# Input projection of a hybrid RWKV-7 / short-convolution block: other columns for the split weights, other pieces, and two pieces in turns

## The chip, the cores and the metric

The kernel runs on one core of one Trainium2 chip. The metric is the time of one execution on the device, in microseconds (us). Before the change the median of three runs is 1019.06 us (1018.99 to 1020.0). Times inside a run come from the hardware profiler's record of one execution.

## The reference

The layer prepends 16 learned tokens to 512 real ones (528 positions, model width 2048), normalises, and multiplies by one input matrix with 8320 columns. Group A (r, k, v, a gate g and two low-rank columns, here "lora") goes through a token shift and a delta-rule recurrence over 16 heads; group B (B, C, h and a gate gc) through a width-3 causal convolution. Both go through one output projection, a residual and a last norm.

```python
hn = _rmsnorm(h_res, norm_in_g[l])
P = hn @ w_in[l]                                   # (528, 2048) @ (2048, 8320)
...
y_a = (yn + bonus.reshape(bsz, L, D_RWKV)) * jax.nn.silu(g_r)
...
y_b = Bg * _causal_depthwise_conv(Cg * hc, conv_w[l]) * jax.nn.silu(g_c)
mix = jnp.concatenate([y_a, y_b], axis=-1)
h_res = h_res + mix @ w_out[l]
out = _rmsnorm(h_res, norm_f_g)
```

Everything is float32.

## The kernel before

**Precision.** A float32 product is made of three matmuls on a reduced format (fp32r): both operands are split into a high part and a low remainder, and high x high, high x low and low x high are added up in PSUM. `xh` and `xl` are the parts of the normalised input, kept in SBUF for the whole projection; they are laid out as [128, 16, 576], one row of 576 columns for each of the 16 blocks of 128 input features, of which columns 0 to 527 hold the positions (0 to 15 the learned tokens).

**Tiles of the projection.** The 8320 output columns make 65 tiles of 128: eight each of r, k, v, g, B, C, h, gc, and one lora. A tile is the product of its 2048 x 128 weights with the input: 16 blocks of features x 3 products. The weights are the stationary operand, the input is the moving one. The positions that a kind needs are cut into pieces, each with its own PSUM bank: `FULL` (k, v, lora) is 0 to 256 and 256 to 528, `TAIL` (r, g, C, h; these start two positions ahead of the first real one) is 14 to 270 and 270 to 528, `REAL` (B, gc) is one piece of 512 from 16 on. So a tile has 96 matmuls, or 48 for B and gc.

**Weights.** `prefetch` (lines 142 to 150 of the kernel) loads half a tile's weights by DMA and has them split in quarters of four feature blocks: ScalarE writes the high part (line 138), VectorE or GpSimd the low one (line 139). `parts_of` puts both into one SBUF tile of 1088 columns, six of which rotate: the high part takes 512 columns from a starting column `SHIFT[kind]` on, the low part the 512 after it. `SHIFT` is thus the place of the weights in their tile, in columns of 4 bytes; it changes nothing in what is computed. For the output projection the same tiles hold the moving operand, at `SHIFT["out"]`.

**Order.** The order on TensorE is written out by hand. `mains` is a generator over the tiles in the order of `plan`; its first stretch runs lora 0, k 0, r 0 and B 0 block by block together, and from the fifth tile on each tile goes through `main`. `main` runs over the four quarters; in each, `steps` runs the first piece over four blocks and three products (12 matmuls, line 326), then the second piece under the same weights again. Every matmul that is yielded adds an estimate of 0.43 ns a column to a clock; small work of the recurrence is put in between by `fill(ns)`, which draws tiles from `mains` until the estimate is used up, and deferred DMAs are issued by the same clock. The first block of lora (line 484) is the one place where the two pieces follow each other under the same weights. After a tile its PSUM banks are read by VectorE (`scaled`, line 345). `pm` rotates four banks for the tiles.

**After the projection** the output product runs over units of 24 matmuls of 512 columns (line 1231), with its own weights prefetched, added and split on the way; the last gc tile's result is needed for it.

Of the kernel before, what the change touches and what calls it, by code (L numbers as in the profile page):

```python
# [18 lines left out]
P = 128  # L19
DM = 2048  # L20
KT = DM // P
SEQ = 512
META = 16
L = SEQ + META
# [50 lines left out]


LX = 576
SHIFT = {"lora": 16, "k": 16, "v": 32, "r": 30, "C": 30, "h": 62, "B": 16, "g": 30, "gc": 0, "out": 40}


@with_exitstack
def hymba_kernel(ctx: ExitStack, tc: tile.TileContext, xt, xtok, front, w_in, w_out, pv, lup, cst, msk, gf, out):
    nc = tc.nc
# [39 lines left out]
    quarters, chain, low = {}, {}, {}  # L123
# [4 lines left out]
    def parts_of(kind, name):  # L128
        t = wp.tile([P, 2 * 512 + 64], F32R, tag="hl", name=name, bufs=6)
        o = SHIFT[kind]  # L130
        return t[:, o : o + 512], t[:, o + 512 : o + 1024]

    def kind_of(j):
        return "out" if j >= N_IN else plan[j % 4 if j < 8 else j // 2][0]
# [7 lines left out]
    def prefetch(upto):  # L142
        while state["next"] < min(upto, len(stream) if chain else N_IN):
            j = state["next"]
            raw = chain[j - N_IN] if j >= N_IN else wp.tile([P, 1024], F32, tag="raw", name=f"wr{j}", bufs=3)
            state["dma"] = nc.sync.dma_start(raw, stream[j]).ins
            with tc.high_priority(offset=WEIGHTS):
                for q in range(2):
                    split_w(2 * j + q, raw[:, q * 512 : (q + 1) * 512], nc.gpsimd if q and 10 < j < N_IN else nc.vector)
            state["next"] = j + 1  # L150
# [6 lines left out]
    xh = xp.tile([P, KT, LX], F32R, name="xh")  # L157
    xl = xp.tile([P, KT, LX], F32R, name="xl")
# [18 lines left out]
    def tm(name):  # L177
        return tp.tile([P, LP], F32, tag="tm", name=name, bufs=3)
# [118 lines left out]
    with tc.issue_after(head):  # L297
        nc.vector.tensor_scalar(
            out=omm, in0=pvt[:, V_MU : V_MU + 33], scalar1=-1.0, scalar2=1.0, op0=ALU.mult, op1=ALU.add
        )  # L300
        for d, off in (
# [4 lines left out]
                out=d, in0=pvt[:, off : off + 8], scalar1=0.5, scalar2=None, op0=ALU.mult  # L306
            )
        nc.vector.tensor_scalar(
            out=hv[:, 4], in0=pvt[:, V_KA : V_KA + 8], scalar1=-0.5, scalar2=1.0, op0=ALU.mult, op1=ALU.add
# [1 line left out]

    nc.scalar.copy(ones, cs[:, C_BM : C_BM + P + 2])
    FULL = ((0, 256), (256, L))
    TAIL = ((14, 270), (270, L))
    REAL = ((META, L),)

    def steps(ps, ranges, k4, q, ks=range(4), rs_=range(2)):
        hi, lo = quarters[q]
        for r, (a, b) in enumerate(ranges):
            if r not in rs_:  # L320
                continue
            for k in ks:
                kt = 4 * k4 + k
                w = slice(k * P, (k + 1) * P)
                for n, (ww, xx) in enumerate(((hi, xh), (hi, xl), (lo, xh))):
                    nc.tensor.matmul(  # L326
                        ps[r], ww[:, w], xx[:, kt, a:b], start=(kt == 0 and n == 0), stop=(kt == KT - 1 and n == 2)
                    )
                    yield (b - a) * 0.43

    def banks(ranges, name, pool, tag):
        return [pool.tile([P, b - a], F32, tag=tag, name=f"ps_{name}_{r}") for r, (a, b) in enumerate(ranges)]

    def main(j, ranges, name):
        prefetch(2 * j + 4)
        ps = banks(ranges, name, pm, "main")
        for k4 in range(4):
            if k4 == 1:
                prefetch(2 * j + 5)
            yield from steps(ps, ranges, k4, 4 * j + k4)  # L340
        return ps

    def scaled(ranges, ps, dst, base):
        for (a, b), p in zip(ranges, ps):
            nc.vector.tensor_tensor(out=dst[:, a - base : b - base], in0=p, in1=rs[:, a:b], op=ALU.mult)
# [12 lines left out]
    def shift_real(ps, m, name, dst):  # L358
        pr = tp.tile([P, L + 1], F32, tag="pr", name=f"pr_{name}", bufs=2)
        scaled(TAIL, ps, pr, 14)  # L360
        sh = tm(f"sh_{name}")[:, 0:SEQ]
# [26 lines left out]
    def behind_of(what):  # L388
        return tc.issue_after(state.pop(what)) if what in state else nullcontext()

    def use(what, i, ps):
# [14 lines left out]
        elif what == "C":  # L406
            u = tm(f"u{i}")
            scaled(TAIL, ps, u, 14)
            got[what, i] = u
        elif what == "h":  # L410
            u = got["C", i]
            hh = tm(f"hh{i}")
            with behind_of("turned"):
                scaled(TAIL, ps, hh, 14)
            n = SEQ + 2
# [56 lines left out]
    def mains():  # L472
        pa = banks(FULL, "lora", pm, "main")
        pb = banks(FULL, "k0", pz, "tz")
        pc = banks(TAIL, "r0", pm, "main")
        pd = [pi.tile([P, SEQ], F32, tag="ser", name="ps_B0")]
        four = ((pa, FULL), (pb, FULL), (pc, TAIL), (pd, REAL))
        for k in range(4):
# [29 lines left out]
        for j in range(4, len(plan)):  # L508
            what, i = plan[j]
            rg = FULL if what in ("k", "v") else REAL if what in ("B", "gc") else TAIL  # L510
            ps = yield from main(j, rg, f"{what}{i}")
            if what == "gc" and i < 4:
                state["split"] = low[4 * j + 4]
            use(what, i, ps)
# [692 lines left out]
    def here(t, n):  # L1207
        return xa[t][:, n * 512 : (n + 1) * 512] if n < 2 else xb[n - 2][:, t]
# [100 lines left out]
    for half in range(2):  # L1309
        o = 28 * half  # L1310
        for g in range(4):
            b = o + 4 + 4 * g
# [43 lines left out]
    for u, unit in enumerate(units):  # L1356
        half, prod, g = unit
# [53 lines left out]
    with tc.manual_schedule(engines={mybir.EngineType.DVE, mybir.EngineType.Activation, mybir.EngineType.Pool}):  # L1411
# [16 lines left out]
        for part in range(2):  # L1428
            cols = slice(256 * part, 256 * part + 256)
            for jj in range(8):  # L1430
                hi, lo = right[(1, "M2", jj // 2), jj % 2]
# [4 lines left out]
            h = here(1, 2)[:, cols]  # L1436
# [70 lines left out]
```

## Time and profile before

| | |
|---|---|
| profiled execution | 1019.06 us, span of its instructions 1017.3 us |
| TensorE busy | 1003.7 us, 9723 matmuls and as many weight loads |
| VectorE, ScalarE, GpSimd busy | 675.5, 393.5, 270.6 us |
| TensorE, 54 to 850 us: waits that the profile shows | 0.7 us |
| one tile without anything between: k, v, C, h | 11.54, 11.77, 11.51, 11.57 us (96 matmuls) |
| the same for B, gc | 10.88, 11.00 us (48 matmuls) |

Matmuls are pipelined: the duration of one in the records (280 to 290 ns for 256 columns) is a latency, and what counts is the distance from one start to the next. It is read from the chain of waits, where a row such as `PE ps_k L326 x96` with its length covers a whole tile, by dividing the length by the count. "PEld" is the weight load, which overlaps the matmul before it.

### The profile page before, as it was taken

Reading aid. Unit: us, or ns where it says so; the run is one execution under the profiler, and the core shown is the slowest. Engines: PE = TensorE matmul, PEld = TensorE weight load, DVE = VectorE, ACT = ScalarE, POOL = GpSimd, SP = SyncE. Lnnn points to the kernel's source line nnn. Section 1 sums busy time; section 2 is a strip of 40 time slices with the busy share of each in tenths; the row PEclk is TensorE's granted clock in tenths of the full one; section 3 lists DMA queues with packets and bytes.
Section 4 is the critical chain, followed back from the end, with each engine's and each line's share of the span. In section 5 each row is a group of like instructions: output and inputs, shape, how many; then the busy total and the mean of one; then the engine's idle time right before and its main releaser. Section 6 shows DMA issues by size and latency. Waiting matters only on the chain.

```text
span 1017.3 us, 23682 instructions
## 1 busy us (share of the span) xinstructions
PE 1003.7 (99%) x9723; PEld 921.5 (91%) x9723; DVE 675.5 (66%) x1239; ACT 393.5 (39%) x729; POOL 270.6 (27%) x292
## 2 busy tenths in 40 slices
PE   9999999999999999999999999999999999999996
PEld 8999998999998999998999998889889898787875
DVE  7786855588665669554668553244555697998787
ACT  7553423344313434322434323222222335445453
POOL 0122514223123323222323222123332332015001
PEclk9999999999999999999999999999999999999998
DMA  9426485546665264853264746877663687695744
GB/s 324 152 82 152 134 210 147 149 124 164 163 158 164 91 168 104 211 148 117 85 178 108 200 139 185 295 224 226 222 206 94 186 272 193 171 327 134 177 124 166
DMA packets 185036, 174.82 MB, mean 172 GB/s; under 512 B 121568, under 2 KB 142816, under 8 KB 184416
## 3 DMA queue, kind: packets, MB, share of 16 engines
q1 hardware_dynamic: 182336, 164.40, 55.4%
q0 software_dynamic: 2304, 8.39, 4.7%
q8 instruction: 76, 1.25, 0.5%
q10 hardware_dynamic: 288, 0.52, 0.1%
q14 instruction: 32, 0.26, 0.1%
HBM read 136.92 MB, written 36.35 MB: 170 GB/s over the span
## 4 chain that ended last, share of the span: by engine, by line
PE 84%; DVE 9%; DMA 3%; issue 2%; ACT 1%; SPq 0%; POOL 0%; DVEq 0%; ACTq 0%; POOLq 0%
PE ps_v L326 9%; PE ps_g L326 9%; PE ps_k L326 9%; PE ps_h L326 9%; PE ps_r L326 9%; PE ps_B L326 9%; PE ps_gc L326 8%; PE ps_C L326 8%; DVE o L1204 3%; DMA wo<-in_w_out_dram 2%; PE g L671 2%; PE M L1231 2%; PE ps_lora L326 1%; PE zs L996 1%; PE zy L1000 1%
## 5 line engine op out<-in xcount | busy, mean ns | idle before, releaser
L138 ACT CAST w<-wr 128x512 fp32r<-128x512 f32 x252 | 153.3, 619 | 304.0 <-PE ps_C L326 53.0
L139 POOL TENSOR_TENSOR w<-wr,w 128x512 fp32r<-128x512 f32 x119 | 159.6, 1342 | 380.9 <-ACT w L138 315.6
L139 DVE TENSOR_TENSOR w<-wr,w 128x512 fp32r<-128x512 f32 x133 | 96.7, 733 | 112.2 <-ACT w L138 101.9
L326 PE MATMUL ps_v<-xh,w 128*128 128x272 f32 (+1 forms) x512 | 96.8, 286 | 0.0
L326 PE MATMUL ps_r<-xh,w 128*128 128x256 f32 (+1 forms) x512 | 96.7, 283 | 0.0
L326 PE MATMUL ps_h<-xh,w 128*128 128x258 f32 (+1 forms) x512 | 96.4, 285 | 0.0
L326 PE MATMUL ps_k<-xh,w 128*128 128x256 f32 (+1 forms) x512 | 95.7, 284 | 0.0
L326 PE MATMUL ps_C<-xh,w 128*128 128x258 f32 (+1 forms) x512 | 95.0, 284 | 0.0
L326 PE MATMUL ps_g<-xh,w 128*128 128x258 f32 (+1 forms) x512 | 93.5, 283 | 0.0
L326 PE MATMUL ps_B<-xh,w 128*128 128x512 f32 x256 | 83.4, 394 | 0.0
L326 PE MATMUL ps_gc<-xh,w 128*128 128x512 f32 x256 | 82.2, 396 | 0.2 <-DVE w L139 0.2
L326 PEld LDWEIGHTS ps_h<-xh,w 128*128 128x128 f32 x512 | 80.2, 189 | 1.1 <-issue 0.4
L326 PEld LDWEIGHTS ps_r<-xh,w 128*128 128x128 f32 x512 | 80.9, 189 | 0.3
L326 PEld LDWEIGHTS ps_v<-xh,w 128*128 128x128 f32 x512 | 80.3, 188 | 0.3
L326 PEld LDWEIGHTS ps_k<-xh,w 128*128 128x128 f32 x512 | 80.0, 189 | 0.5
L326 PEld LDWEIGHTS ps_C<-xh,w 128*128 128x128 f32 x512 | 79.9, 189 | 0.6
L326 PEld LDWEIGHTS ps_g<-xh,w 128*128 128x128 f32 x512 | 79.5, 189 | 0.3
L326 PE MATMUL ps_v<-xl,w 128*128 128x256 f32 (+1 forms) x256 | 73.1, 286 | 0.0
L326 PE MATMUL ps_h<-xl,w 128*128 128x256 f32 (+1 forms) x256 | 72.4, 283 | 0.3 <-issue 0.3
L326 PE MATMUL ps_k<-xl,w 128*128 128x256 f32 (+1 forms) x256 | 72.6, 283 | 0.0
L326 PE MATMUL ps_r<-xl,w 128*128 128x256 f32 (+1 forms) x256 | 72.5, 283 | 0.0
L326 PE MATMUL ps_g<-xl,w 128*128 128x256 f32 (+1 forms) x256 | 72.5, 283 | 0.0
(321 smaller groups left out, 2267.6 us busy)
## 6 DMA issues: line engine op xcount, KB each, us to landing
wr<-in_w_in_dram SPq DMA_DIRECT2D x126, 512.0 KB
ct<-opd SPq DMA_DIRECT2D x64, 288.0 KB
wo<-in_w_out_dram SPq DMA_DIRECT2D x24, 512.0 KB
x<-in_w_out_dram POOLq DMA_DIRECT2D x16, 512.0 KB, 6.0
opd<-ar SPq DMA_DIRECT2D x8, 576.0 KB
opd<-gt SPq DMA_DIRECT2D x16, 288.0 KB
opd<-bt SPq DMA_DIRECT2D x64, 64.0 KB
x<-in_w_out_dram SPq DMA_DIRECT2D x8, 512.0 KB
```

What stands on the lines that cost most here:

```text
L138: nc.scalar.copy(hi, rq)
L139: low[q] = eng.tensor_tensor(out=lo, in0=rq, in1=hi.bitcast(F32), op=ALU.subtract).ins
L326: nc.tensor.matmul(ps[r], ww[:, w], xx[:, kt, a:b], start=(kt == 0 and n == 0), stop=(kt == KT - 1 and n == 2))
L671: nc.tensor.matmul(z[h][:, c - c0], bk[hs, c, h : h + 2, :].rearrange("p a s -> p (a s)"), ar[hs, c].rearrange("p a s -> p (a s)"), start= ...
L996: nc.tensor.matmul(d[hs, j], w, x[hs], start=(a == 0), stop=(a == b - 1))
L1000: nc.tensor.matmul(d[ho, j], t[hs, o : o + CH], x[hs], start=(a == 0), stop=(a == b - 1))
L1204: nc.vector.tensor_tensor(out=lo, in0=rq, in1=hi.bitcast(F32), op=ALU.subtract)
L1231: nc.tensor.matmul(bank[s], left(prod, jj, m, s), w, start=(jj == 0 and n == 0), stop=(jj == 7 and n == 2))
```

## The change

Three things. In `SHIFT`, the weights of v go from column 32 to 16, of gc from 0 to 16, of r and g from 30 to 32, of h from 62 to 32, of C from 30 to 64; lora, k, B and the output weights stay. The pieces of r, g, C and h are cut at 272 instead of 270, so the first has 258 columns and the second 256. And in tiles of k, r and h, in the first three of the four quarters, the two pieces take turns: each of the 12 steps of a quarter is done for the first piece and then for the second, before the next step. The last quarter keeps the old order, and so does the first stretch of `mains`. The number of matmuls, weight loads, DMAs and evictions is what it was.

```diff
-SHIFT = {"lora": 16, "k": 16, "v": 32, "r": 30, "C": 30, "h": 62, "B": 16, "g": 30, "gc": 0, "out": 40}
+TURNS = "k", "r", "h"
+SHIFT = {"lora": 16, "k": 16, "v": 16, "r": 32, "C": 64, "h": 32, "B": 16, "g": 32, "gc": 16, "out": 40}
...
-    TAIL = ((14, 270), (270, L))
+    TAIL = ((14, 272), (272, L))
...
+    def by_turns(ps, ranges, k4, q):
+        hi, lo = quarters[q]
+        for k in range(4):
+            kt = 4 * k4 + k
+            w = slice(k * P, (k + 1) * P)
+            for n, (ww, xx) in enumerate(((hi, xh), (hi, xl), (lo, xh))):
+                for p, (a, b) in zip(ps, ranges):
+                    nc.tensor.matmul(
+                        p, ww[:, w], xx[:, kt, a:b], start=(kt == 0 and n == 0), stop=(kt == KT - 1 and n == 2)
+                    )
+                    yield (b - a) * 0.43
+
     def main(j, ranges, name):
...
-            yield from steps(ps, ranges, k4, 4 * j + k4)
+            turns = len(ranges) == 2 and k4 < 3 and kind_of(2 * j) in TURNS
+            yield from (by_turns if turns else steps)(ps, ranges, k4, 4 * j + k4)
```

## The prediction

> **What bounds the kernel now.** I read the busy time by engine first, then the throttle's row, then the chain of waits in order of time, then the waits of TensorE.
>
> ```profile
> span 1017.3 us, 23682 instructions
> PE 1003.7 (99%) x9723; PEld 921.5 (91%) x9723; DVE 675.5 (66%) x1239; ACT 393.5 (39%) x729; POOL 270.6 (27%) x292
> ...
> PEclk9999999999999999999999999999999999999998
> ```
>
> TensorE is busy 99% of the span at the full granted clock, and every matmul has a weight load of its own (9723 and 9723), also where two matmuls in a row use the same weights. The waits of TensorE between 54 and 850 us, where nearly all of the input projection runs, are these three and no more:
>
> ```profile
> PE ps_h L326 <- issue: 0.3, 1, 0.3
> PE rz L944 <- DMA ct<-opd: 0.2, 1, 0.2
> PE ps_gc L326 <- DVE w L139: 0.2, 1, 0.2
> ```
>
> So there is no stall to remove; only the matmuls' own spacing can change. The chain of waits gives that spacing wherever a whole tile ran with nothing in between (start, length, name, count; 96 matmuls for two pieces, 48 for one):
>
> ```profile
> 386.76 11.77 PE ps_v L326 x96
> 425.22 11.51 PE ps_C L326 x96
> 474.63 11.54 PE ps_k L326 x96
> 794.51 11.00 PE ps_gc L326 x48
> 805.50 11.51 PE ps_C L326 x96
> 817.01 11.57 PE ps_h L326 x96
> 828.58 10.88 PE ps_B L326 x48
> ```
>
> r and g have no undisturbed tile; their longest runs stand in for one:
>
> ```profile
> 224.26 6.96 PE ps_r L326 x58
> 266.47 6.95 PE ps_g L326 x58
> ```
>
> Divided out, ns per matmul: k 120.2, v 122.6, C 119.9, h 120.5, r 120.0, g 119.8, B 226.7, gc 229.2. k and v run the same pieces (256 and 272 columns, 264 on average) on the same data; in the program only the column at which their weights stand differs, 16 against 32. B and gc run the same 512 columns, weights at 16 against 0. So where the weights stand is worth 2.4 and 2.5 ns of a matmul.
>
> To compare tiles of other widths I need the price of a column: B and k, both at column 16, give (226.7 - 120.2) / (512 - 264) = 0.43 ns. r, g, C and h average 257 columns, 7 fewer than k and v. At k's rate they would take 120.2 - 3.0 = 117.2 ns (11.25 us a tile), at v's 119.6 (11.48). They take 119.8 to 120.5: **today they pay v's dear rate or a little more**, though the distance from their weights to their data is k's (30 - 14 and 30 - 270 against 16 - 0 and 16 - 256; 16 and -240 in both). What sets them apart from k is that 14, 270, 30 and 62 are no multiples of 16 columns.
>
> **The change part by part.**
>
> *Weights of v from 32 to 16.* v becomes k in every respect: 11.77 - 11.54 = 0.23 us a tile, 8 tiles, **-1.84 us**.
>
> *Weights of gc from 0 to 16.* gc becomes B: 11.00 - 10.88 = 0.12 us, 8 tiles, **-0.96 us**. Some of gc's matmuls wait for weights (0.2 us above), which doesn't change.
>
> *r, g, h: weights to column 32, pieces 14 to 272 and 272 to 528.* The number of columns stays 514, so the swap of 256 and 258 costs nothing by itself. The second piece now starts at 272, a multiple of 16, with its weights at 32 and the distance 32 - 272 = -240, k's exactly; I give it k's rate. The first piece still starts at 14, with the distance 18; no row shows such a pair, so I bound it by k's rate (a gain as large as the second piece's) and by v's excess of 2.4 ns on top of today's (a loss), and take no change, since its start is what it was. So half of the way from today's tile to 11.25 us: r (11.52 - 11.25) / 2 = 0.135, g (6.95 / 58 x 96 = 11.50) 0.125, h 0.16 us a tile; 8 tiles each: **-1.08, -1.00, -1.28 us**. Bounds for the three: -6.7 us with both pieces at k's rate; +5.5 us (24 tiles x 0.23) with column 32 as dear for them as it is for v.
>
> *C: weights to column 64, the same pieces.* Its distances become 50 and -208; -208 and gc's old 0 - 16 differ by a multiple of 64, and gc's is the dear one. I take v's rate for the second piece: (11.51 - 11.48) / 2 = 0.015, times 8, **-0.12 us**. Bounds: -2.1 us (k's rate, 8 x 0.26) and +1.9 us (gc's excess of 2.5 ns on 768 matmuls).
>
> *Turns in k, r, h.* In three of four quarters of a tile the order becomes first piece, second piece under the same weights. The first stretch of the program runs its own order, so k and r have 7 such tiles and h has 8: 22 x 72 = 1584 matmuls. No instruction is added, and since each matmul keeps its own weight load, none is saved. The trace has one sample of this order: the very first block of lora is written that way (weights at column 16, pieces of 256 and 272).
>
> ```profile
> 4.41 1.21 PE L484 MATMUL ps_lora<-xh,w 128*128 128x256 f32 x4
> 5.46 0.40 PE L484 MATMUL ps_lora<-xl,w 128*128 128x256 f32 x2
> 5.70 0.28 PE L326 MATMUL ps_k<-xh,w 128*128 128x256 f32 x1
> ...
> 6.43 0.29 PE L326 MATMUL ps_r<-xh,w 128*128 128x256 f32 x1
> 6.55 0.28 PE L326 MATMUL ps_r<-xl,w 128*128 128x256 f32 x1
> 6.67 0.40 PE L326 MATMUL ps_r<-xh,w 128*128 128x256 f32 x2
> ```
>
> The last two matmuls in turns take 5.70 - 5.46 = 0.24 us, 120 ns each, k's rate without turns (120.2). **0 us.** From one pair read to 0.01 us the error is some 5 ns, so the bounds are wide: below, -2.5 ns each (the whole distance between v and k, -4 us); above, each turn might cost as much as the change of tile does in r's rows, 120 ns for the second matmul against 6.55 - 6.43 = 0.12 for the first, that is under 10 ns by rounding; I take 5 (+8 us).
>
> In turns the second piece's PSUM bank is written from a quarter's second matmul on, 11 matmuls (1.3 us) sooner than before. That bank was last used two to four pieces back, at least a whole tile (10.9 us) ago, and VectorE frees a finished tile quickly:
>
> ```profile
> 806.48 0.68 DVE L345 TENSOR_TENSOR gc<-ps_gc,rs 128x512 f32<-128x512 f32 x1
> 818.09 0.42 DVE L345 TENSOR_TENSOR u<-ps_C,rs 128x256 f32<-128x256 f32 x1
> 819.90 0.42 DVE L345 TENSOR_TENSOR u<-ps_C,rs 128x258 f32<-128x258 f32 x1
> ```
>
> gc, done at 805.50, was read by 807.2, and C, done at 817.01, by 820.3. So 3.3 us of 10.9 are used, the earlier need is covered, and without that cover it would cost at most 1.3 us a tile. The two C rows also show that an eviction of 258 columns takes as long as one of 256. What writes the weights doesn't care where they stand: over seven different columns ScalarE's conversion lies within 34 ns.
>
> ```profile
> L138 ACT CAST w<-wr x252: 602/621/636, 21.9 to 837.9; 128x512 fp32r<-128x512 f32 x126
> ```
>
> The order of all other work follows a count of estimated time in which a matmul of 256 or 258 columns counts 110 or 111 ns, so what is interleaved moves by one matmul at most: 0.
>
> *Does it reach the end?* VectorE's work between projection and output product is released by the last gc matmul:
>
> ```profile
> 850.49 0.69 DVE L345 TENSOR_TENSOR gc<-ps_gc,rs 128x512 f32<-128x512 f32 x1 [1.41 <-PE ps_gc L326]
> ```
>
> VectorE had been idle for 1.41 us there, so it starts earlier by what TensorE saves. The DMA of the recurrence's first chunk (0.2 us of wait above) may swallow a few tenths.
>
> Sum: -1.84 - 0.96 - 1.08 - 1.00 - 1.28 - 0.12 + 0 = -6.3 us. The profiled execution took 1019.06 us, its span 1017.3 and 1.8 around it; it is also the median of the runs (1018.99 to 1020.0). 1019.06 - 6.3 = **1012.8**, rounded to **1013**.
>
> **Skill and trace.** The Trainium skill (TensorE: Matmul & The Clock Gate, "Step-by-step: what each phase is for") says that TensorE reads weights and moving data through two independent SBUF ports, so that loading the next weights takes nothing from the running matmul. By that rule no column matters, and the sum would be 0. The trace doesn't agree: k and v differ by 0.23 us a tile. What it would do here is rival 3.
>
> **The rivals.**
>
> 1. *Both pieces reach k's rate.* If a multiple of 16 for weights and distance is all that counts, r, g, h and C all fall to 11.25 us: 8 x (0.27 + 0.25 + 0.32 + 0.26) = 8.8, with v and gc 11.6: 1007.5 us. For it: today's distance is right and yet the rate is dear. Against: the first piece still starts at column 14.
> 2. *Only v and gc move.* r, g, h and C stay where they are (1016.3) or come to v's rate (8 x (0.04 + 0.02 + 0.09 + 0.03) = 1.4 more, 1014.9). For it: v shows column 32 with aligned data at 119.6 ns, next to what they pay today.
> 3. *The change doesn't do what it says.* The difference between k and v is not the column but, say, what the other engines do in their stretches; then nothing moves and the time stays 1019.06. Against: B and gc repeat the difference with other neighbours.
> 4. *Multiples of 32 are the dear columns* (the other side). The two dear kinds stand at 32 and 0, the cheap ones at 16; after the change r, g, h stand at 32 and C at 64. If that adds to what the start at column 14 costs: 24 x 0.23 + 1.9 = +7.4, less 2.8: 1023.7 us. It decides from 2.8 us over 32 tiles, 0.9 ns a matmul. Against: r, g and h already pay as much as v.
> 5. *Turns cost.* From 6.3 us / 1584 = 4 ns a matmul the gain is gone; at 5 ns 1021 us. Against: the pair in lora's first block.
>
> **How the numbers follow.** Forecast 0.46 (its own range 1010 to 1016), rival 1 0.12, rival 2 0.22, rival 3 0.07, rival 4 0.08, rival 5 0.05. The range 1007.4 to 1018 takes in the forecast and the first two rivals, 0.80, and leaves out the last three. About 0.2%, 2 us, is what can be told from no change. Faster: 0.46 + 0.12 + 0.21 = 0.79. Same: rival 3 and edges of 2 and 5, 0.10. Slower: rival 4 and most of 5, 0.11.
>
> **What would show it.** v tiles of 11.54 us and gc tiles of 10.88 confirm the first two steps. For r, g and h, the pieces of 256 at 272 should be spaced 3 ns closer than before and the pieces of 258 as their width says; both closer means rival 1, neither rival 2, both wider rival 4. k's weights and pieces don't change, so its tiles show the turns alone: 11.54 us if they are free. I would be wrong outright if v kept 11.77, if a k tile changed by more than 0.2 us, or if the tiles got shorter and the waits for the output weights grew by as much.

## The result and the profile after

The changed kernel takes 1011.91 us (median of six, 1011.16 to 1012.89) against 1019.02 us for the kernel before in the same comparison: a ratio of 0.9931, 95% interval 0.9918 to 0.9943. That is 7.1 us less; 6.3 were forecast.

The head of the page of the changed kernel, whose profiled execution took 1011.85 us:

```profile
span 1010.0 us, 23678 instructions
PE 996.3 (99%) x9723; PEld 914.1 (90%) x9723; DVE 680.8 (67%) x1239; ACT 393.6 (39%) x729; POOL 284.3 (28%) x292
...
PEclk9999999999999999999999999999999999999999
```

The same matmuls and weight loads at the same clock, still 99% busy: the 7.3 us of span went out of the spacing, not out of waits. GpSimd (POOL) has grown by 13.7 us, to which I return. The tiles in the chain of waits of the changed kernel (start, length, name, count; a tile of k or h in turns shows its first 72 matmuls, since the last quarter is another line of the program):

```profile
384.23 11.58 PE ps_v L327 x96
422.08 11.20 PE ps_C L327 x96
470.85 8.64 PE ps_k L343 x72
798.57 11.39 PE ps_C L327 x96
809.95 8.48 PE ps_h L343 x72
821.25 10.90 PE ps_B L327 x48
832.15 10.90 PE ps_gc L327 x48
```

v fell from 11.77 to 11.58, gc from 11.00 to B's 10.90, C from 11.51 to 11.20 or 11.39. h runs at 8.48 / 72 = 117.8 ns a matmul (120.5 before), k at 120.0 (120.2 before). The waits of TensorE between 54 and 850 us:

```profile
PE ps_gc L327 <- DVE w L140: 0.6, 1, 0.6
PE ps_h L343 <- issue: 0.3, 1, 0.3
```

The wait for the recurrence's first chunk is gone, one wait for weights has grown from 0.2 to 0.6 us. And the gain reaches the end whole: VectorE reads the last gc tile 7.42 us sooner than before (850.49), and from there to the end it is 166.9 us against 166.8.

```profile
843.07 0.69 DVE L360 TENSOR_TENSOR gc<-ps_gc,rs 128x512 f32<-128x512 f32 x1 [1.38 <-PE ps_gc L327]
```

For the pieces one by one I took the distance from each matmul's start to the next one's over the whole trace: the mean in ns, first and second piece of each kind (k and v 256 and 272 columns; r, g, C, h 256 and 258, or 258 and 256 where the cut is at 272). The first stretch and distances that hold a wait (over 150 ns, for 512 columns over 270) are left out. Rows are the two kernels and the experiments below.

```
                                k             v             r             g             C             h             B            gc
before                116.9 123.6   118.9 126.6   120.6 119.8   120.0 119.7   120.0 119.8   120.3 120.7         227.8         229.5
after                 116.4 124.1   117.1 123.7   120.1 116.8   120.3 115.9   119.6 115.8   119.9 116.7         228.1         227.8
e1_v_gc               117.6 123.6   116.2 123.6   120.6 119.8   120.2 119.7   119.9 119.8   120.3 120.7         227.8         227.7
e2_cut                117.0 123.6   119.0 126.5   119.8 118.0   119.9 117.9   119.8 117.8   120.2 117.9         228.5         229.3
e3_columns            117.2 123.5   119.0 126.5   119.8 119.8   120.1 119.9   119.9 119.8   119.9 119.8         227.9         229.2
e4_no_turns           117.7 123.5   116.8 123.6   120.1 115.9   120.3 115.8   119.7 115.3   120.6 115.4         228.1         227.6
e5_turns_all          116.4 124.2   116.2 124.2   120.1 116.8   120.4 116.9   118.9 117.8   119.9 116.8         228.2         227.7
e6_after_again        116.5 124.1   117.1 123.7   120.1 116.8   120.3 115.9   119.7 115.8   119.8 116.6         228.1         227.6
e7_other_columns      118.9 125.5   117.8 126.2   119.8 119.3   120.1 118.3   120.4 115.7   119.7 115.5         232.8         233.3
e8_starts             117.5 123.5   117.2 123.6   119.9 114.4   122.0 115.8   119.6 116.1   121.3 114.7         228.2         227.4
e9_turns_k            116.4 124.2   116.7 123.6   120.2 115.5   120.3 115.9   119.6 115.8   120.6 115.4         228.1         227.6
e10_no_turns_again    117.6 123.5   116.9 123.6   120.2 115.7   120.3 115.8   119.7 115.3   120.6 115.3         228.1         227.5
e11_turns_alone       116.4 124.1   118.9 126.6   120.4 121.0   120.1 119.7   120.0 119.8   119.1 121.2         227.9         229.3
```

One row repeats to 0.1 or 0.2 ns between runs of the same kernel (after and e6, e4 and e10); k and v, where their part of the program is the same in several kernels, differ by up to 1.0 ns on the piece of 256 between them, so a single cell of two different kernels is read to about 1 ns. Nor is a cell always one spacing: it is a mean over tiles that can stand at different levels. In the changed kernel without turns (e4) the pieces of 256 at 272 stand at 113.3 ns in every quarter of C's first four tiles and at 117.5 to 118.0 in three of the last four; C's cell of 115.3 lies between the two. (Tiles are numbered from 0 within their kind, in the order in which they run; where a tile's time below stands in no row of a chain, it is added up from the means of its distances in this way.)

The projection's own distances, summed from the first v tile to the end of the projection, went from 709.1 to 701.6 us. I count what a distance over the limits above has beyond 0.43 ns a column plus 7 ns as a break, and the rest as spacing. The spacing went from 696.9 to 688.9 us, 7.9 less, the breaks from 12.2 to 12.7. Most of the breaks (some 115 in each kernel) are passages to the recurrence's products and back, of about 0.1 us; the profile lists 0.5 us of them as waits before, 0.9 after.

### The profile page after: what moved, and what is told of

It is laid out like the page before. It is cut to its first block, busy times and chain, and to the rows that moved or that the text cites. A ratio compares the mean times of both kernels' runs of the same rounds, so it can differ in the third digit from the quotient of the medians.

```text
span 1010.0 us, 23678 instructions
## 1 busy us (share of the span) xinstructions
PE 996.3 (99%) x9723; PEld 914.1 (90%) x9723; DVE 680.8 (67%) x1239; ACT 393.6 (39%) x729; POOL 284.3 (28%) x292
## 4 chain that ended last, share of the span: by engine, by line
PE 87%; DVE 7%; DMA 2%; issue 2%; ACT 1%; POOL 0%; DVEq 0%; SPq 0%; ACTq 0%; POOLq 0%
PE ps_v L327 9%; PE ps_C L327 9%; PE ps_g L327 9%; PE ps_B L327 9%; PE ps_gc L327 8%; PE ps_h L343 7%; PE ps_k L343 6%; PE ps_r L343 6%; PE ps_k L327 3%; PE ps_r L327 3%; PE M L1246 3%; DVE o L1219 2%; PE ps_h L327 2%; PE g L686 2%; DMA wo<-in_w_out_dram 1%
## 5 line engine op out<-in xcount | busy, mean ns | idle before, releaser
L327 PE MATMUL ps_C<-xh,w 128*128 128x256 f32 (+1 forms) x512 | 93.3, 281 | 0.0
L327 PE MATMUL ps_g<-xh,w 128*128 128x256 f32 (+1 forms) x512 | 92.0, 281 | 0.0
L327 PE MATMUL ps_g<-xl,w 128*128 128x258 f32 (+1 forms) x256 | 72.3, 282 | 0.0
L327 PE MATMUL ps_C<-xl,w 128*128 128x258 f32 (+1 forms) x256 | 71.8, 280 | 0.0
L327 PEld LDWEIGHTS ps_gc<-xh,w 128*128 128x128 f32 x256 | 47.7, 188 | 11.2 <-DVE w L140 1.1
L343 PE MATMUL ps_r<-xh,w 128*128 128x258 f32 x336 | 57.1, 281 | 0.0
L327 PEld LDWEIGHTS ps_B<-xh,w 128*128 128x128 f32 x256 | 47.7, 188 | 10.1 <-DVE w L140 0.4
L343 PE MATMUL ps_k<-xh,w 128*128 128x256 f32 x336 | 56.0, 284 | 0.0
L327 PE MATMUL ps_B<-xl,w 128*128 128x512 f32 x128 | 50.4, 393 | 0.0
L327 PE MATMUL ps_gc<-xl,w 128*128 128x512 f32 x128 | 50.3, 393 | 0.0
```

The lines of the kernel that those rows point to most:

```text
L327: nc.tensor.matmul(ps[r], ww[:, w], xx[:, kt, a:b], start=(kt == 0 and n == 0), stop=(kt == KT - 1 and n == 2))
L343: nc.tensor.matmul(p, ww[:, w], xx[:, kt, a:b], start=(kt == 0 and n == 0), stop=(kt == KT - 1 and n == 2))
```

## The experiments

### The columns of v and gc alone

```diff
-SHIFT = {..., "v": 32, ..., "gc": 0, ...}
+SHIFT = {..., "v": 16, ..., "gc": 16, ...}
```

> The kernel before, with only the weights of v at column 16 instead of 32 and of gc at 16 instead of 0. Theory (the place of the weights relative to the moving data sets the spacing): v tiles go from 11.77 to 11.55 us, gc tiles from 11.00 to 10.90, nothing else moves; the time falls by 8 x (0.22 + 0.10) = 2.6 us, to 1016.4 (ratio 0.9974). Rival (columns of weights don't matter, k and v differed for another reason): v tiles stay at 11.77, time 1019.0.

Measured: 1016.64 us against 1019.07, ratio 0.9975 (0.9966 to 0.9985), 2.4 us less. The chain of waits of this kernel:

```profile
385.72 11.53 PE ps_v L326 x96
...
473.24 11.58 PE ps_k L326 x96
...
803.23 11.51 PE ps_C L326 x96
814.74 11.57 PE ps_h L326 x96
826.31 10.88 PE ps_B L326 x48
837.20 10.90 PE ps_gc L326 x48
```

v is now as short as k and gc as B, C and h are what they were. An edit of two numbers that moves weights and nothing else shortens the very tiles whose weights it moves: where the weights stand counts, and "another reason than the column" (rival 3) is out.

### The cut alone, and the columns of r, g, h and C alone

```diff
-    TAIL = ((14, 270), (270, L))
+    TAIL = ((14, 272), (272, L))
```

> The kernel before, with only the cut of r, g, C, h at 272 instead of 270 (weights stay at 30, 30, 30, 62). Theory (both weights and piece must start at multiples of 16 columns): the pieces of 256 that now start at 272 stay at about 120 ns a matmul, because the weights still don't start at such a multiple; time within 0.7 us of 1019.0. Rival (only the start of the moving data counts): these pieces fall to 116 to 117 ns, 1536 matmuls x 3.5 ns less 1536 x 0.5 for the wider first pieces, 4.6 us, time 1014.4.

```diff
-SHIFT = {..., "r": 30, "C": 30, "h": 62, ..., "g": 30, ...}
+SHIFT = {..., "r": 32, "C": 64, "h": 32, ..., "g": 32, ...}
```

> The kernel before, with only the weights of r, g, h at column 32 and of C at 64; the cut stays at 270, v and gc stay where they were. Theory (both must start at multiples of 16 columns): the second pieces, starting at 270, stay at about 120 ns; time within 0.7 us of 1019.0. Rival (only the weights' column counts): second pieces, and first ones too, fall by 2 to 4 ns, 3 to 12 us in all, time 1007 to 1016.

Measured: the cut alone 1016.46 us, ratio 0.9974 (0.9962 to 0.9985); the columns alone 1018.28 us, ratio 0.9994 (0.9985 to 1.0003), no difference that can be told. The chain of the first, then of the second:

```profile
802.55 11.40 PE ps_C L326 x96
813.95 11.44 PE ps_h L326 x96
```

```profile
805.19 11.50 PE ps_C L326 x96
816.70 11.51 PE ps_h L326 x96
```

My theory that both starts are needed falls in part. With weights at columns 30 and 62, off any multiple of 16, the pieces at 272 still fell from some 120 to 118 ns; the rival that only the start of the data counts expected 116 to 117. With weights at 32 and 64 but pieces at 270, nothing falls, as the theory said. The table shows the rest when both are there (e4): 115.3 to 115.9. So for these pieces the start of the data is worth about 2 ns by itself, the weights' columns nothing by themselves and about 2 ns more on top of the cut.

In times: v and gc -2.4, cut -2.6, columns -0.8, together -5.8 us; the kernel with all of it and no turns is 8.6 us faster than before (next). Some 2.7 us come from cut and columns acting together. Each of the four times is known to about 1 us, so this rest is known to about 2; the table gives 2.4 us for it (the pairs of r, g, C and h in e4 against e2, less e3 against the kernel before).

The gain from the weights' columns comes as a level that some tiles reach and others don't. With the cut alone C's eight tiles lie between 11.39 and 11.41 us, with their second pieces near 117.8 ns; with the columns too (e4) three of the last four still take 11.38 or 11.39 us, the first four 11.20.

### Without the turns

```diff
-TURNS = "k", "r", "h"
+TURNS = ()
```

> The changed kernel without the turns: k, r and h run the first piece of a quarter and then the second, as all other tiles do. In the changed kernel, pieces of 256 of r and h take 117.1 to 117.5 ns in the three quarters in turns and 114.7 to 115.5 in the last one, which has none. Theory (turns cost on these pieces): without turns they take about 115.5 ns everywhere, 36 x 15 matmuls x 1.8 ns = 1.0 us less, the pieces of 258 about 0.3 ns more; time 1011.9 - 0.8 = 1011.1, k tiles unchanged at 11.54 us. Rival (turns helped, which the sum over pieces would show): time 1012.5 or more, and r and h tiles longer than in the changed kernel.

Measured: 1010.51 us against 1019.07, ratio 0.9916 (0.9903 to 0.993). Its chain:

```profile
222.80 6.82 PE ps_r L327 x58
264.53 6.82 PE ps_g L327 x58
...
469.91 11.57 PE ps_k L327 x96
...
570.63 11.20 PE ps_C L327 x96
...
808.20 11.29 PE ps_h L327 x96
```

r and g run at 6.82 / 58 = 117.6 ns (120.0 and 119.8 before). In the table a pair of pieces in r takes 236.0 ns without turns and 236.9 with them, in h 236.0 and 236.6; restricted to the three quarters that are in turns, 235.6 against 237.8 in r and 235.8 against 236.8 in h. The piece of 256 at 272 has 117.1 to 117.5 ns in turns and 115.2 to 115.4 without, but a distance in turns runs from one piece to the other, and in h the first piece fell meanwhile from 120.5 to 119.8; the pair is what counts. The spacing of the projection sums to 688.2 us without turns and 688.9 with; the breaks are 12.0 and 12.7. So the turns lose 0.7 us in spacing and 0.7 in breaks, of which the profile lists 0.5 as waits. The interval of this ratio and that of the changed kernel (0.9918 to 0.9943) overlap; that the turns cost time rests on the two traces as much as on the times, and on the pair of runs further below.

Nor do all tiles lose. h's tiles 0 to 3 and 7 take 11.29 to 11.32 us with turns and without; the loss is in tiles 4 to 6, most in 5 (11.48 against 11.33). r's tiles 4 to 7 take 11.36 us against 11.30 or 11.31.

### Turns in all tiles of two pieces, beside the changed kernel

```diff
-TURNS = "k", "r", "h"
+TURNS = "k", "r", "h", "v", "g", "C"
```

> The changed kernel with turns in v, g and C as well. Without turns, r and h took 115.2 to 115.8 ns for their pieces of 256, with them 117.1 to 117.5, and the kernel without turns took 1010.5 us against 1011.9. Theory (turns cost about 2 ns on a piece of 256 that starts at 272, nothing to speak of elsewhere): g and C rise from 116 to 117.5, v stays at 117 / 123.7; 2 x 8 x 36 x 1.6 ns = 0.9 us more, 1012.8. Rival (turns cost nothing, the difference of the two runs was another): g and C stay at 116, 1011.9.

> The changed kernel once more, beside the one with turns everywhere on the same chip: 1011.9 us by both theories; it is the measure for the others.

Measured on one chip: turns everywhere 1012.59 us, the changed kernel 1011.52 us, each against 1018.69 (ratios 0.9945, 0.9931 to 0.9959, and 0.9933, 0.9919 to 0.9947). The chain with turns everywhere:

```profile
384.30 8.64 PE ps_v L343 x72
...
572.13 8.52 PE ps_C L343 x72
...
799.23 8.55 PE ps_C L343 x72
```

The size was about as the theory said, 1.1 us more, though by the intervals the two times alone can't be told apart. The place shows in the tiles: three quarters of this C tile take 8.52 us in turns, against 0.75 x 11.20 = 8.40 for the same tile without, and the pair of pieces rose from 236.2 to 237.3 ns in g and from 235.4 to 236.7 in C. v doesn't mind: 8.64 against 0.75 x 11.58 = 8.69. Nor does a C tile that stood at the dear level: the last one takes 8.55 us, 0.75 x 11.39 = 8.54 without turns. In turns all eight C tiles take 11.34 to 11.39 us, so what the turns cost C is the level of 11.20.

### Turns in k alone, beside the kernel without turns

```diff
-TURNS = "k", "r", "h"
+TURNS = "k",
```

> The changed kernel with turns in k alone. In k a pair of pieces took 116.1 + 124.2 ns in turns and 117.6 + 123.5 without, 0.8 ns less, over 7 tiles of 36 such pairs 0.2 us. Theory (turns lose in r and h, gain a little in k): 0.2 us under the kernel without turns, 1010.3, and r and h at 115.5 and 120.3 ns as without turns. Rival (the kernel without turns was faster for another reason than the spacing in r and h): 1011.5, as with all three in turns.

> The changed kernel without turns once more, beside the one with turns in k alone, on the same chip: 1010.5 us by both theories.

Measured on one chip: 1010.72 and 1010.71 us, each against 1018.88 (ratios 0.9918, 0.9904 to 0.9931, and 0.9917, 0.9903 to 0.993). The spacing of r and h is back at 115.5 and 115.4 ns for the pieces of 256, and the median at that of the kernel without turns; this speaks against the rival, whose 1011.5 us the interval alone (up to 1011.9) doesn't shut out. The 0.2 us that k was to win is not to be seen, but it is also less than the two times can tell. The chain has k at 8.64 / 72 = 120.0 ns against 11.57 / 96 = 120.5 (e4), and k's tiles are 0.15 us shorter in all. Yet the spacing of the whole projection is 688.1 us in both runs: the first C tile, which is the same in both kernels, has lost about as much. Its rows with turns in k and without:

```profile
131.66 11.38 PE ps_C L327 x96
```

```profile
131.99 11.20 PE ps_C L327 x96
```

The weights' column, the pieces and the order of this tile are the same, and in the changed kernel it also takes 11.38 us. So column and start alone don't fix the spacing; what ran before counts too. And a wait has grown (first the kernel with turns in k, then the one without):

```profile
PE ps_gc L327 <- DVE w L140: 0.6, 1, 0.6
```

```profile
PE ps_gc L327 <- DVE w L140: 0.2, 1, 0.2
```

It is the first gc tile, at 161 us, which waits for its low weights. In every run with turns in k this wait is 0.6 us; in those without it is 0.2 us or too short to be listed. VectorE writes those weights behind other work in that stretch; that a shift of the order there by a matmul or two makes it later is likely, but I didn't test it.

### Turns alone, on the kernel before

The function and the two lines of `main` are added; `SHIFT` and `TAIL` stay those of the kernel before.

> The kernel before with the turns alone; columns and cut stay as they were. Theory (what turns cost in r and h is the good spacing of a piece that starts at 272 with its weights at 32; where both pieces are dear, there is nothing to lose): r and h stay at 120 ns within 0.5 for both pieces, k loses 0.4 ns a matmul; time 1018.9 within 0.7. Rival (changing pieces costs by itself): r and h rise by about 1 ns on both pieces, 1.1 us over 1080 turned matmuls, time 1020.

Measured: 1020.07 us against 1018.88, ratio 1.0011 (1.0002 to 1.002). The chain:

```profile
475.94 8.65 PE ps_k L342 x72
...
817.48 8.64 PE ps_h L342 x72
```

The time is the rival's, the spacing fits neither: r's second piece rose from 119.8 to 121.0 with the first unchanged, h's first fell by 1.2 ns and its second rose by 0.5, and h takes 8.64 / 72 = 120.0 ns in the chain against 120.5. Over the projection the spacing sums to 697.0 us against 696.9, the breaks to 12.6 against 12.2. The profile thus shows about half a microsecond of the 1.2; the rest lies within the interval (0.2 to 2.0 us) and within what one execution differs from another (its output part took 167.8 us against 167.0). What is settled is that turns bring nothing, with the old columns or the new.

### Eight other columns

```diff
-SHIFT = {"lora": 16, "k": 16, "v": 16, "r": 32, "C": 64, "h": 32, "B": 16, "g": 32, "gc": 16, "out": 40}
+SHIFT = {"lora": 16, "k": 0, "v": 48, "r": 16, "C": 32, "h": 64, "B": 48, "g": 48, "gc": 32, "out": 40}
```

with no turns.

> The changed kernel without turns, with eight other columns for the weights, all multiples of 16: k 0, v 48, r 16, g 48, h 64, C 32, B 48, gc 32. Theory (with both starts at multiples of 16, a piece of 256 or 272 is cheap when weights and piece stand an odd multiple of 16 columns apart, a piece of 512 when an even one): on pieces of 256, k (distance 0) goes from 117.6 to 119, its 272 from 123.5 to 126.5; v (48) stays at 117 and 123.6; r (16 - 272 = -256) and g (-224) go from 115.5 to 118; h (-208) and C (-240) stay at 115.5; B (32) stays at 227.7, gc (16) goes from 227.6 to 229.5. Rival (the weights' own column counts, 16 being the cheap one): r is the cheapest, and k, v, g, h, C and B, gc all become dearer. Time by the theory: 1010.5 + 0.5 (k, 256) + 1.1 (k, 272) + 1.0 + 1.0 (r, g) + 0.7 (gc) = 1014.8.

Measured: 1018.79 us against 1018.69, ratio 1.0 (0.9991 to 1.001): with every column still a multiple of 16, the whole gain of 8 us is gone. The chain:

```profile
386.90 11.73 PE ps_v L327 x96
...
474.45 11.72 PE ps_k L327 x96
...
804.87 11.41 PE ps_C L327 x96
816.27 11.38 PE ps_h L327 x96
827.66 11.19 PE ps_B L327 x48
838.85 11.21 PE ps_gc L327 x48
```

For pieces of 256 the distance rule held in all six kinds, with cells dear against cheap: k at distance 0 118.9 (117.6 at 16), r at -256 119.3 and g at -224 118.3 (115.8 at -240), C at -240 and h at -208 115.7 and 115.5, v at 48 117.8 (116.8 at 16, 118.9 at 32; these are 1 ns apart, no more than a cell is read to). For the others it fell: the 272 columns of v take 126.2 ns at column 48 though -208 is an odd multiple of 16, and 512 columns take 227.6 with weights at 16, 229.5 at 0, 232.8 at 48 and 233.3 at 32. There one column of four is good, not every second. These three come to 4.5 us, somewhat more than the 4.0 by which my forecast of 1014.8 missed: B 5.1 ns x 384 = 2.0 us, gc 3.8 x 384 = 1.5, v's second piece 2.6 x 384 = 1.0. The rival, that the weights' own column counts whatever the data, falls with r, which at 16 is the dearest of its group.

### Other starts of the first piece

```diff
+BEGIN = {"r": 12, "g": 8, "h": 10, "C": 14}
...
-            rg = FULL if what in ("k", "v") else REAL if what in ("B", "gc") else TAIL
+            rg = FULL if what in ("k", "v") else REAL if what in ("B", "gc") else ((BEGIN[what], 272), (272, L))
```

with no turns; the added leading columns of a piece are computed and skipped by the eviction.

> The changed kernel without turns, with another start of the first piece, whose extra columns are computed and not read: r starts at 12 (260 columns), h at 10 (262), g at 8 (264), C stays at 14 (258). Without turns the first pieces at 14 take 119.7 (C) to 120.5 (h) ns. Theory (a start must be a multiple of 16 columns, 64 bytes): all stay dear, and each extra column adds 0.43 ns: r 121.0, h 122.2, g 122.8, so the time rises by 8 x 48 x (0.9 + 1.7 + 2.6) ns = 2.0 us, to 1012.5. Rival (a multiple of 4 columns, 16 bytes, is enough): r and g lose some 3 ns, to 118 and 120, h stays dear at 122; time about 1010. A multiple of 2 being enough would make h cheap too, 119.

Measured: 1012.46 us against 1018.69, ratio 0.994 (0.9926 to 0.9954), the theory's 1012.5. First pieces: 119.9 ns for 260 columns from 12, 121.3 for 262 from 10, 122.0 for 264 from 8, 119.6 for 258 from 14. Taking off 0.43 ns a column leaves 8.1, 8.6, 8.5 and 8.7; the same for the second pieces at 272, 115.3 in the mean, is 115.3 - 110.1 = 5.2. So none of these starts brings the first piece down to the second's price; 12, a multiple of 16 bytes, is half a nanosecond better, not three. The first pieces of k and v, which start at 0, leave 7.4 and 7.1 here. What a first piece of r, g, C or h would cost from a multiple of 16 columns no run tried.

That the time came out as forecast is luck. The spacing of the projection is 688.7 us against 688.2 and 688.1 in the two traces of the kernel without turns, 0.5 more and not 2.0: as r's and h's first pieces grew, their second ones fell to 114.4 and 114.7 ns, and r's tiles, two columns wider, got shorter (11.22 to 11.26 us against 11.30 to 11.40). The rest of the 2 us lies elsewhere. The distances within the projection that start at a product of the recurrence sum to 89.9 us here and to 87.4 and 88.3 there. TensorE's waits between 54 and 850 us in this trace, all of them at such products:

```profile
PE zy L1017 <- issue: 0.6, 2, 0.3
PE t L860 <- DVE xn L851: 0.4, 1, 0.4
PE rz L961 <- DMA ct<-opd: 0.4, 1, 0.4
```

## Why the prediction was right or wrong

*What bounds the kernel* was right: 99% busy before and after, the spacing alone moved, and the order of the tiles carried it through to the end.

*v from 32 to 16*, -1.84: the chain has 11.53 us in e1 (the columns of v and gc alone) and 11.58 in the changed kernel, 1.9 and 1.5 us over eight tiles. Right. *gc from 0 to 16*, -0.96: 10.90 us, 0.8. Right.

*r, g, h*, -3.4: by the table (sum of both cells, 384 pairs a kind) r and g -1.3 each, h -1.7, in all -4.4. The second piece was given k's rate, 117; it does better, 115.3 to 115.9 without turns. The first was to stay as it was but for its width; it stayed as it was with its width: 258 columns take what 256 took. The mechanism held and its size was too small. That both starts must be multiples of 16 to gain anything, as I put it for the cut alone, is refuted by that run, which gained half of it.

*C*, -0.12: **this step failed.** 11.51 fell to 11.20 or 11.39, by the table 4.4 ns a pair, -1.7 us. I took the price of a distance that is dear for gc's 512 columns as the price of the same distance for 256. The eight columns show that the good places depend on the width of the piece: -208 is good for 256 columns at 272, dear for 272 columns at 256.

*Turns*, 0: the step failed too, in the other direction. One pair in lora's first block couldn't show 2 ns, and it was a pair of 256 at 0 and 272 at 256, which is the kind that doesn't mind (k, v); some tiles of r and h do. The cost is some 0.7 us of spacing (r and h 0.5, first C tile 0.2, v 0.1, k -0.2) and, with k's share in the wait of the first gc tile, about 1.2 us in all. That is rival 5 in sign, at a fraction of its price, so the gain outlived it.

*The earlier need of the PSUM bank* showed in no wait. *What is interleaved moves by one matmul at most: 0* was too simple: a wait of 0.2 us became 0.6.

*What writes the weights doesn't care* was right for ScalarE, which I had quoted (393.5 and 393.6 us busy; its row covers five columns, not seven), and wrong for GpSimd, which I had not looked at; see below.

So 6.3 forecast against 7.1 measured is a sum of errors of both signs, and that they partly cancel is luck: by the table C gave 1.6 us and r, g and h (with what the turns cost their spacing already taken off) 1.0 us more than forecast, v (1.8) and gc (0.65) 0.35 us less, and breaks took 0.5. That makes 8.0; the table overstates, since it counts full tiles and r's first tile and the pairs next to a wait are not in it, and the sum over all spacing and breaks is 7.4. Rival 1 (both pieces at k's rate, 2.1 us in C) came near C's size by the wrong mechanism: the second pieces fell, and no first piece by more than 0.5 ns. Rival 4 (multiples of 32 are dear) is out: r and g got their best rate at 32, h at 32 and 64.

The changed kernel without turns is the best of these runs: 1010.5 and 1010.7 us in two comparisons, with ratios of 0.9916 and 0.9917 where the changed kernel had 0.9931 and 0.9933.

By the Trainium skill (TensorE: Matmul & The Clock Gate, "Step-by-step: what each phase is for") weights and moving data come through independent ports, and loading the next weights takes no read bandwidth from the running matmul. The runs differ: a matmul of 512 columns takes 227.6 to 233.3 ns, with nothing of its own changed but the weights' column. What makes the two meet no run here shows; it stays open. So does why the tiles of C in one and the same kernel take 11.20 us in some places and 11.39 in others; the first C tile, which changes from one to the other with the turns in k, shows that it is not the column alone.

## What to carry to other kernels

When TensorE is busy throughout, compare kinds of tiles that should cost the same; a difference of 2% between two of them, with the same shapes, is a lead, and the chain of waits gives it without any experiment. Where operands stand in SBUF is worth trying for each width of matmul by itself: a good distance between weights and data for 256 columns was the worst for 512, and two edits that gained 2.6 and 0.8 us alone (the second no more than the noise) gained some 6 together, taken as the gain without turns less that of v and gc. Read the spacing tile by tile before trusting a mean: one kernel ran tiles of one kind at two levels. And an order that "should be free" needs its own run: without the turns the kernel was 8.6 and 8.2 us faster than before in two comparisons, with them 7.1 and 7.2.

## What the runs showed that I had not expected

GpSimd's half of the weight splits got slower with the columns. The groups of GpSimd on the split's line, in the kernel before, in e1 (v and gc moved), in e3 (r, g, h and C moved) and in the changed kernel (busy us, mean ns of one, then its idle time):

```profile
L139 POOL TENSOR_TENSOR w<-wr,w 128x512 fp32r<-128x512 f32 x119 | 159.6, 1342 | 380.9 <-ACT w L138 315.6 <-issue 45.3 <-DMA opd<-bt 8.9
```

```profile
L139 POOL TENSOR_TENSOR w<-wr,w 128x512 fp32r<-128x512 f32 x119 | 160.6, 1351 | 376.9 <-ACT w L138 322.6 <-issue 45.0 <-DMA ct<-opd 4.9
```

```profile
L139 POOL TENSOR_TENSOR w<-wr,w 128x512 fp32r<-128x512 f32 x119 | 173.1, 1455 | 369.0 <-ACT w L138 305.8 <-issue 44.3 <-DMA opd<-ar 6.0
```

```profile
L140 POOL TENSOR_TENSOR w<-wr,w 128x512 fp32r<-128x512 f32 x119 | 171.6, 1443 | 363.6 <-ACT w L139 313.1 <-issue 42.3 <-DMA mix<-yd 4.1
```

It follows r, g, h and C. Put in order of tiles, the median of one split is 1092 to 1131 ns for weights at columns 30 and 62 (r, g, C, h in the kernel before) and 1282 to 1297 ns at 0, 16 and 32 (k, v, B, gc there); in the changed kernel, with all columns multiples of 16, it is 1288 to 1294 for every kind. So on this engine the columns that are good for TensorE cost 200 ns an instruction, 12 us in all. GpSimd is busy 28% of the span and nothing waits for it here, so it costs no time; in a kernel where GpSimd is the bound the same edit would have lost.
